# Index and value weights of the sparse mixer loaded in the MLP before it, and its small results in a pool of their own

## The chip, the cores and the metric

The kernel runs on one core of one Trainium2 chip. The metric is the device time of one execution in microseconds. The core has five engines that run their own queues of instructions: TensorE (PE, matrix multiply; PEld is its weight load), VectorE (DVE), ScalarE (ACT), GpSimd (POOL) and SyncE (SP), which here issues nearly all DMAs.

## The reference, cut to what matters

A decoder trunk of four residual layers over x of 512 tokens by 1024 channels, float32: an attention-and-SSM mixer, an MLP, a sparse attention mixer (DSA), a second MLP. Each layer ends in a layer norm. The change lies at the border of the first MLP and the DSA mixer, which picks 128 keys for each query before it attends:

```python
proj = x @ w_in                       # q 1024, k 256, v 256, qi 8x32, ki 32, wi 8 columns
rel = relu(einsum('bqhd,bsd->bqsh', qi_b, ki))           # index: 8 heads of 32
score = einsum('bqsh,bqh->bqs', rel, wi_b) * idx_scale
score = where(causal, score, -inf)
_, idx = top_k(score, 128)            # for each query
... softmax attention over the chosen keys, 16 heads, 4 key heads, ALiBi ...
x = layer_norm(ALPHA * x + o @ w_out)
x = layer_norm(ALPHA * x + square(relu(x @ w1)) @ w2)    # MLP, d_ff 4096
```

## The kernel before, in words

Every float32 product is computed in three float32r matmuls: both operands are split into a rounded part (`hi`, a copy on ACT) and the rest (`lo`, a subtraction on DVE or POOL); `mm3` (lines 129 to 133) adds hi·hi, hi·lo and lo·hi. `weights` (line 96) loads 512 KB of weights into a tile `raw` (three in rotation) and splits it into `whi` and `wlo` (four in rotation in the common pool `wp`; the MLP's pool `hp` has four of its own). x stands transposed and split in `xhi`, `xlo`.

A tile scheduler orders the instructions of each engine when the kernel is built; on the chip each engine then runs its own list strictly in that order, and SP its list of DMAs. A tile's next user waits until its last reader is done.

The MLP (`mlp`) computes 32 column blocks of the hidden layer and folds most of the down projection into products of half matrices (`down_chunk`), with a side sum `u`. Its last two groups of four blocks (`up_split`, with a scratch tile `r`) are followed by `mlp_block` for the four token blocks, and each token block's layer norm (`layer_norm`, with scale and shift in `gb`) follows its last product. The norm parameters are loaded at any time after the tile `gb` is free, here early in the MLP.

The DSA mixer starts with `index_scores`. It loads and splits the small weights of ki and wi (`wk`, 64 columns) and two blocks of qi weights, all in `wp`. For each half of the tokens (c = 0, 1; 256 tokens) it computes three projections `psi` (k of the index with wi, then two of its queries), splits them into `hl` tiles (two in rotation), and sends them through DRAM to another layout: `hl` to `kd` and from there to `kist`, `hl` to `qd` and from there to `qist` (three DMAs), all on SP's queue. Then `score_block` runs for the query blocks 1, 2, 3 (256, 384, 512 keys): eight matmuls `psx` (one for each head), each followed by a ReLU on ACT into `rel` (four in rotation) and one accumulation `acc` on DVE (line 1081). Block 0 needs no choice.

`top_keys` (line 1106) finds the 128 largest scores of each query in 16 steps: `vec.max` gives the next eight (MAX8), `vec.match_replace` strikes them out, and each needs the one before it. It runs for block 1 alone, later for blocks 2 and 3 in turns. `project_v1` loads and splits two weight tiles of v and computes it (`psb`, 96 matmuls of 256 columns); then two projections of k and eight of q follow (`psa`), whose weights from the third q on are split on POOL. The attention (`sparse_attention`) begins with query block 2, whose first DVE instruction (line 1143) reads `dist`, the result of `top_keys`.

Of the kernel before, what the change touches and what calls it, by code (L numbers as in the profile page):

```python
# [8 lines left out]
F32 = mybir.dt.float32  # L9
# [26 lines left out]
class Trunk:  # L36
# [59 lines left out]
    def weights(self, srcs, n=1024, eng=None, pool=None, parts=1, tag=None):  # L96

        nc = self.nc
        raw, hi, lo = self.w_tiles(pool, tag)
# [8 lines left out]
    def w_cols(self, w, c0, eng=None, pool=None, tag=None):  # L108
# [4 lines left out]
        hi, lo = self.weights(srcs, eng=eng, pool=pool, tag=tag)  # L113
        return hi.rearrange("p (k c) -> p k c", c=P), lo.rearrange("p (k c) -> p k c", c=P)
# [90 lines left out]
    def mlp(self, w1, w2, g, b, last):  # L205
# [7 lines left out]
        with self.tc.tile_pool(name=self.nm("mlp"), bufs=2, side="right", reuse_waits="tile") as hp:  # L213
# [17 lines left out]
            def up_split(grp):  # L231
                hhi, hlo = h_tile(F32R), h_tile(F32R)
                for f in range(4):
                    ps = self.proj_fm(w1, grp * 512 + f * P, None)
                    h = hp.tile([P, S], F32, tag="r", bufs=1, name=self.nm("r"))
                    nc.scalar.activation(h, ps, AF.Relu)
                    nc.scalar.activation(h, h, AF.Square)
                    nc.scalar.copy(hhi[:, f, :], h)
                    nc.vector.tensor_tensor(hlo[:, f, :], h, hhi[:, f, :].bitcast(F32), ALU.subtract)
                    yield hhi, hlo  # L240

            for hs in up_raw(0, True):
                pass
            u = hp.tile([P, 2, 512], F32, tag="u", bufs=1, name=self.nm("u"))
# [710 lines left out]
    def mixer_dsa(self, w_in, w_out, g, b):  # L955
        nc, tc = self.nc, self.tc
        act, vec, pool = nc.scalar, nc.vector, nc.gpsimd
        with tc.tile_pool(name="m1", bufs=1, reuse_waits="tile") as mp, \
                tc.tile_pool(name="m1d", bufs=1, space=DRAM) as dp, \
# [6 lines left out]
            for h in range(16):  # L966
                pool.memset(sc[64 * (h % 2):64 * (h % 2) + 64, h // 2:h // 2 + 1], -0.125 / slope(h))
            with tc.tile_pool(name="idxs", bufs=1, side="right", reuse_waits="tile") as sp:
                accs, drm = self.index_scores(w_in, ip, sp, dp)
            vec.tensor_copy(dist[:, 0, 0:P], drm[:, S - P:])  # L970
            self.top_keys((1,), ip, accs, drm, dist)
            self.project_v1(w_in, v)
# [8 lines left out]
            with tc.tile_pool(name="att1", bufs=2, side="right", reuse_waits="tile") as ap:  # L981
                attend = lambda m, qb: self.sparse_attention(m, qb, qsts[4 * m:4 * m + 4], ap, kst, v, dist, chi, clo)
                self.top_keys((2, 3), ip, accs, drm, dist)
# [25 lines left out]
    def index_scores(self, w_in, op, ip, dp):  # L1009
# [3 lines left out]
        drm = op.tile([P, S], F32, name="drm")  # L1013
        cm = op.tile([P, S], F32, name="cm")
# [3 lines left out]
        pool.memset(cm, 0.0)  # L1018
        pool.affine_select(out=cm, in_=cm, pattern=[[-1, S]], compare_op=ALU.is_ge, fill=LOW,
                           base=S - P, channel_multiplier=1)  # L1020


        raw, hi, lo = self.w_tiles()
# [8 lines left out]
        wk = [t[:, 0:n].rearrange("p (k c) -> p k c", c=64) for t in (hi, lo)]  # L1032
        wts = [wk] + [self.w_cols(w_in, 1536 + i * P) for i in range(2)]
        wi = op.tile([P, NB, 8], F32, name="wi")

        kst = ip.tile([96, S], F32R, name="kist")
        qst = ip.tile([96, 8, S], F32R, name="qist")
        for c in range(2):
            tok = slice(c * 256, c * 256 + 256)
            kd = dp.tile([2, 32, 256], F32, name="kd", bufs=2)  # L1040
            qd = dp.tile([2, 2 * P, 256], F32, name="qd", bufs=2)
            for i, (hi, lo) in enumerate(wts):
                m = P if i else 64
                ps = (self.abank([P, 256], "psi") if c == 0 or i == 0 else
                      self.psb.tile([P, 256], F32, tag="psb", name=self.nm("psi")))
                for k in range(KT):
                    self.mm3(ps[:m], hi[:, k, :], lo[:, k, :], self.xhi[:, k, tok], self.xlo[:, k, tok],
                             k == 0, k == KT - 1)
                rows = slice(0, P) if i else slice(32, 64)
                hl = self.hl_tile()[:, :, 0:256]  # L1050
                self.split(hl[rows, 0, :], hl[rows, 1, :], ps[rows])
                if i == 0:
                    nc.sync.dma_start(kd.rearrange("a d t -> d a t"), hl[rows].bitcast(F32))
                    wiT = ip.tile([8, S], F32, tag="rel", bufs=4, name=self.nm("wiT"))[:, 0:256]
                    act.activation(wiT, ps[0:8], AF.Copy, scale=0.0625)
                else:
                    nc.sync.dma_start(qd[:, (i - 1) * P:i * P, :].rearrange("a d t -> d a t"), hl.bitcast(F32))
            nc.sync.dma_start(kst[0:64, tok].bitcast(F32), kd.rearrange("a d t -> (a d) t"))
            nc.sync.dma_start(kst[64:96, tok].bitcast(F32), kd[0])
            for r in range(3):  # L1060
                nc.sync.dma_start(qst[32 * r:32 * r + 32, :, tok].bitcast(F32),
                                  qd[r // 2].rearrange("(h d) t -> d h t", d=32))
# [3 lines left out]
            act.copy(wi[:, 2 * c:2 * c + 2, :], ps)  # L1066
        accs = [None] + [self.score_block(qb, wi, qst, kst, cm, op, ip) for qb in (1, 2, 3)]
        return accs, drm

    def score_block(self, qb, wi, qst, kst, cm, op, ip):  # L1070

        nc = self.nc
        nk = (qb + 1) * P
        qs = slice(qb * P, (qb + 1) * P)
        acc = op.tile([P, S], F32, tag="acc", bufs=3, name=self.nm("acc"))[:, :nk]
        for h in range(8):
            ps = self.abank([P, S], "psx")
            nc.tensor.matmul(ps[:, :nk], qst[:, h, qs], kst[:, :nk], start=True, stop=True)
            r = ip.tile([P, S], F32, tag="rel", bufs=4, name=self.nm("rel"))[:, :nk]
# [3 lines left out]
        return acc  # L1083

    def project_v1(self, w_in, v):

        nc = self.nc
        ws = []
        for i in range(2):
# [4 lines left out]
            ws += [(hi[:, k, :], lo[:, k, :]) for k in range(4)]  # L1094
        for t in range(NB):
# [10 lines left out]
    def top_keys(self, qbs, ip, accs, drm, dist):  # L1106

        vec = self.nc.vector
        for step in range(TOPK // 8):
            for qb in qbs:  # L1110
                acc = accs[qb]
                top = ip.tile([P, 8], F32, tag="top", bufs=1, name=self.nm("top"))
# [42 lines left out]
    def run(self):  # L1155
# [3 lines left out]
        self.mlp(a["w1"][0], a["w2"][0], g[1:2], b[1:2], False)  # L1159
# [42 lines left out]
```

## Time and profile before

| | us |
|---|---|
| median of 3 runs | 1166.77 (1166.69 to 1170.47) |
| the profiled execution | 1165.24 |
| its span, first to last instruction | 1163.5 |
| PE busy in the span | 1108.7 (95%) |
| DVE busy | 841.5 (72%) |
| ACT busy | 532.4 (46%) |
| POOL busy | 173.1 (15%) |

The profile is of one execution; it gives for each engine what ran when, and what ended its idle time. A busy PE counts matmuls in its pipeline. PE is nearly always busy, so the places where it stands still are what to look for: the chain of work that ended last runs over PE for 80% of the span and over DVE for 12%. The first MLP ends at about 590 us, the index runs to about 652 us, the attention from 698 to 790 us.

### The profile page before, as it was taken

The page shows a single profiled execution, that of the slowest core. Times are in us where ns is not written, and L with a number is a line of the kernel's source. Part 1 is how long each engine was busy: PE and PEld are TensorE (multiplying, and loading weights), DVE is VectorE, ACT ScalarE, POOL GpSimd, SP SyncE. Part 2 cuts the span into 40 slices and gives each one's busy share as a digit, 9 for nine tenths or more (in the row PEclk, how much of TensorE's full clock was granted, in tenths as well). Part 3 has the DMA queues.
Part 4 walks back from the last instruction along what each step waited for, and adds up shares of the span by engine and source line. Part 5 has one row for each costly group of instructions (what it writes and reads, how often), then busy time and mean ns, then how long its engine had stood idle before and what let it go on. Part 6 is the DMA issues. An engine that isn't in the chain of part 4 may idle for free.

```text
span 1163.5 us, 15569 instructions
## 1 busy us (share of the span) xinstructions
PE 1108.7 (95%) x5860; PEld 923.6 (79%) x5860; DVE 841.5 (72%) x1255; ACT 532.4 (46%) x832; POOL 173.1 (15%) x201
## 2 busy tenths in 40 slices
PE   7988998999999999999999959998999999999997
PEld 6877876788888888888888847776988888888886
DVE  7997598694666866975668997538548668587736
ACT  5534387324444544554135427642445445445510
POOL 1043230320000000000021744325000000000001
PEclk9999999999999999999999989999999999999999
DMA  7526683751242242333056850025304414415101
GB/s 244 142 64 156 188 220 100 211 151 37 72 145 91 75 150 66 110 108 79 1 141 160 217 164 1 19 69 186 109 19 127 129 35 145 127 38 162 37 1 73
DMA packets 147307, 126.99 MB, mean 109 GB/s; under 512 B 24353, under 2 KB 115297, under 8 KB 147233
## 3 DMA queue, kind: packets, MB, share of 16 engines
q1 hardware_dynamic: 145552, 123.59, 36.7%
q10 hardware_dynamic: 1680, 2.41, 0.6%
q8 instruction: 46, 0.75, 0.3%
q14 instruction: 29, 0.23, 0.1%
HBM read 105.80 MB, written 5.37 MB: 96 GB/s over the span
## 4 chain that ended last, share of the span: by engine, by line
PE 80%; DVE 12%; DMA 3%; issue 2%; ACT 2%; SPq 1%; POOLq 0%; DVEq 0%; ACTq 0%
PE psa L133 11%; PE psa L132 11%; PE psa L131 11%; PE psb L313 7%; PE psb L311 7%; PE psb L312 7%; PE pso L949 3%; PE psb L382 3%; PE psb L381 3%; PE psb L380 2%; PE pst L942 2%; DVE acc L1114 2%; DVE top L1113 2%; PE psb L841 2%; PE psb L842 2%
## 5 line engine op out<-in xcount | busy, mean ns | idle before, releaser
L133 PE MATMUL psa<-xhi,wlo 128*128 128x512 f32 (+1 forms) x720 | 267.1, 372 | 0.0
L132 PE MATMUL psa<-xlo,whi 128*128 128x512 f32 (+1 forms) x720 | 266.6, 371 | 0.0
L131 PE MATMUL psa<-xhi,whi 128*128 128x512 f32 (+1 forms) x720 | 265.6, 371 | 0.2 <-ACT xhi L202 0.2
L104 ACT CAST whi<-raw 128x1024 fp32r<-128x1024 f32 (+1 forms) x129 | 133.3, 1046 | 200.9 <-PE psa L132 130.1
L105 DVE TENSOR_TENSOR wlo<-raw,whi 128x1024 fp32r<-128x1024 f32 (+1 forms) x102 | 127.8, 1258 | 80.5 <-ACT whi L104 79.7
L132 PEld LDWEIGHTS psa<-xlo,whi 128*128 128x128 f32 x720 | 135.7, 188 | 23.4 <-DVE xlo L203 0.4
L133 PEld LDWEIGHTS psa<-xhi,wlo 128*128 128x128 f32 x720 | 135.8, 189 | 23.1
L131 PEld LDWEIGHTS psa<-xhi,whi 128*128 128x128 f32 x720 | 135.0, 188 | 23.1 <-ACT xhi L202 0.5
L299 DVE TENSOR_TENSOR wlo<-b,whi 128x1024 fp32r<-128x1024 f32 x84 | 102.5, 1221 | 43.0 <-ACT whi L298 42.8
L311 PE MATMUL psb<-whi,whi 128*128 128x512 f32 x336 | 130.7, 389 | 0.0
L312 PE MATMUL psb<-wlo,whi 128*128 128x512 f32 x336 | 130.7, 389 | 0.0
L313 PE MATMUL psb<-whi,wlo 128*128 128x512 f32 x336 | 129.7, 389 | 0.0
L298 ACT CAST whi<-b 128x1024 fp32r<-128x1024 f32 x84 | 88.3, 1051 | 42.0 <-PE psb L313 30.2
L105 POOL TENSOR_TENSOR wlo<-raw,whi 128x1024 fp32r<-128x1024 f32 x27 | 70.8, 2632 | 132.5 <-ACT whi L104 131.4
L184 POOL TENSOR_TENSOR rs<-rs,two 128x1 f32<-128x1 f32 x16 | 22.7, 1417 | 423.8 <-DVE rs L183 423.8
L312 PEld LDWEIGHTS psb<-wlo,whi 128*128 128x128 f32 x336 | 63.1, 188 | 13.2
L313 PEld LDWEIGHTS psb<-whi,wlo 128*128 128x128 f32 x336 | 63.1, 188 | 13.1
L311 PEld LDWEIGHTS psb<-whi,whi 128*128 128x128 f32 x336 | 63.1, 188 | 13.0
L293 DVE TENSOR_TENSOR b<-b,b 128x1024 f32<-128x1024 f32 x48 | 63.1, 1320 | 11.4 <-DMA b<-in_w_dram 10.9
L298 ACT CAST whi<-h 128x1024 fp32r<-128x1024 f32 x36 | 38.0, 1054 | 54.0 <-PE psb L312 34.0
L299 DVE TENSOR_TENSOR wlo<-h,whi 128x1024 fp32r<-128x1024 f32 x36 | 43.9, 1220 | 14.0 <-ACT whi L298 13.5
L841 PE MATMUL psb<-whi,xhi 128*128 128x512 f32 x128 | 51.5, 410 | 0.8 <-DVE x L848 0.6
(263 smaller groups left out, 1955.4 us busy)
## 6 DMA issues: line engine op xcount, KB each, us to landing
raw<-in_w_dram SPq DMA_DIRECT2D x80, 512.0 KB, 4.1
b<-in_w_dram SPq DMA_DIRECT2D x48, 512.0 KB, 4.5
raw<-in_w_in_dram SPq DMA_DIRECT2D x29, 512.0 KB, 4.5
raw<-in_w_out_dram SPq DMA_DIRECT2D x16, 512.0 KB, 4.8
qst<-hl SPq DMA_DIRECT2D x48, 128.0 KB, 3.5
kst<-hl SPq DMA_DIRECT2D x24, 256.0 KB, 4.7
gb<-in_ln_g_dram SPq DMA_DIRECT2D x4, 512.0 KB, 4.1
gb<-in_ln_b_dram SPq DMA_DIRECT2D x4, 512.0 KB, 5.0
```

The costliest lines, as they stand in the source:

```text
L104: nc.scalar.copy(hi[:, c], raw[:, c])
L105: (eng or nc.vector).tensor_tensor(lo[:, c], raw[:, c], hi[:, c].bitcast(F32), ALU.subtract)
L131: mm(ps, lhi, rhi, start=start, stop=False)
L132: mm(ps, lhi, rlo, start=False, stop=False)
L133: mm(ps, llo, rhi, start=False, stop=stop)
L293: vec.tensor_tensor(o, p, q, op)
L298: act.copy(hi, src)
L299: vec.tensor_tensor(lo, src, hi.bitcast(F32), ALU.subtract)
L311: mm(ps, lh, bhi[:, k, :], start=i + k == 0, stop=False)
L312: mm(ps, lh, blo[:, k, :], start=False, stop=False)
L313: mm(ps, ll, bhi[:, k, :], start=False, stop=i + k == 2)
L841: nc.tensor.matmul(ps, chi[:, k, tok], whi, start=i == 0, stop=False)
```

## The change

Six things are done, all around the border of the two layers:

- A new pool `idx0` is opened before the first MLP (`index_open`) with `drm` (distances), `kist`, `wi` and `acc1`, the scores of query block 1. `drm` is filled before the MLP.
- `index_early`, called at the MLP's last group, loads and splits the three weight tiles of the index into tiles of the MLP's pool (tags `b22`, `b12`, `b11`), and the two of v into `wp`. `index_projections` is called before the MLP's pool closes.
- Within it, for c = 0 only 128 tokens of the queries are projected (block 1; block 0 is never scored), and the scores of block 1 are computed at once, before the second half of the tokens.
- The split results lie in one tile `hls` for each half (two places, used in turn by the three projections) instead of the rotating `hl`.
- The tile `cm` with the causal bias goes; `score_block` fills each `acc` by one DVE instruction from `drm` and always adds to it.
- In both MLPs `u` and `r` share the one tile of `gb` (`ur`; `r` now has two places), so the norm parameters can be loaded only when both are no longer read.

```diff
-    def mlp(self, w1, w2, g, b, last):
+    def mlp(self, w1, w2, g, b, last, early=None):
...
-                    h = hp.tile([P, S], F32, tag="r", bufs=1, name=self.nm("r"))
+                    h = r[:, f % 2, :]
...
+            ur = self.cp.tile([P, 2, D], F32, tag="gb", bufs=1, name=self.nm("ur"))
+            u, r = (ur[:, i, :].rearrange("p (h c) -> p h c", c=512) for i in range(2))
...
-            u = hp.tile([P, 2, 512], F32, tag="u", bufs=1, name=self.nm("u"))
...
+                    then = early(hp) if early else None
...
+            if early:
+                then()
...
+    def index_open(self):
+        ip = self.ix = self.ctx.enter_context(self.tc.tile_pool(name="idx0", bufs=1, side="right"))
+        self.dp = self.ctx.enter_context(self.tc.tile_pool(name="m1d", bufs=1, space=DRAM))
+        self.drm = ip.tile([P, S], F32, name="drm")
+        self.kist = ip.tile([96, S], F32R, name="kist")
+        self.wi = ip.tile([P, NB, 8], F32, name="wi")
+        self.acc1 = ip.tile([P, 256], F32, name="acc1")
...
+    def index_early(self, w_in, hp):
...
+        def tiles(tag):
+            raw = self.wp.tile([P, 1024], F32, tag="raw", bufs=3, name=self.nm("raw"))
+            return raw, *(hp.tile([P, 1024], F32R, tag=tag, bufs=2, name=self.nm("wx")) for _ in range(2))
...
+        wts += [self.w_cols(w_in, 1536 + i * P, tiles=tiles(tag)) for i, tag in enumerate(("b12", "b11"))]
+        self.vw = self.v1_weights(w_in)
+        return lambda: self.index_projections(wts, hp)
...
+            hls = hp.tile([P, 2, 2, 256], F32R, tag="b21", bufs=2, name=self.nm("hls"))
+            rel = hp.tile([P, 4, 256], F32, tag="s4", bufs=1, name=self.nm("rel"))
...
+                n = P if i and c == 0 else 256
+                at = slice(tok.stop - n, tok.stop)
...
-                hl = self.hl_tile()[:, :, 0:256]
+                hl = hls[:, i % 2, :, 0:n]
...
+            if c == 0:
+                qst = hp.tile([P, 1024], F32R, tag="b21", bufs=2, name="qist1")[0:96].rearrange(
+                    "p (h t) -> p h t", t=P)
+                self.load_index_queries(qst, P)
+                slots = itertools.count()
+                self.score_block(1, qst, self.acc1, lambda: rel[:, next(slots) % 4, :])
...
-            nc.vector.scalar_tensor_tensor(acc, r, wi[:, qb, h:h + 1], acc if h else cm[:, S - nk:],
-                                           ALU.mult, ALU.add)
+        nc.vector.tensor_scalar(acc, self.drm[:, S - nk:], BIG, LOW, ALU.is_ge, ALU.mult)
...
+            nc.vector.scalar_tensor_tensor(acc, r, self.wi[:, qb, h:h + 1], acc, ALU.mult, ALU.add)
...
+        self.index_open()
+        self.mlp(a["w1"][0], a["w2"][0], g[1:2], b[1:2], False, lambda hp: self.index_early(a["w_in1"], hp))
```

The scheduler then orders each engine anew. PE's list is the same, shape by shape, outside the index. Three places of the lists follow. SP, the index's DMAs, before (kd, qd: stores to DRAM of the index's k and queries; kist, qist: loads of them in the other layout; raw: weights):

```order
L1057 DMA qd<-hl_5104 128x2x256
L1061 DMA qist<-qd 32x8x256 x3
L101 DMA raw_5588<-in_w_in_dram 128x8x128
L1053 DMA kd<-hl_5144 32x2x256
L101 DMA raw_5629<-in_w_in_dram 128x8x128
L1057 DMA qd<-hl_5175 128x2x256
L1058 DMA kist<-kd 64x256
L1059 DMA kist<-kd 32x256
L101 DMA raw_5670<-in_w_in_dram 128x8x128
L1057 DMA qd<-hl_5204 128x2x256
L1061 DMA qist<-qd 32x8x256 x3
```

and now:

```order
L1084 DMA qd<-hls_4991 128x2x128
L1102 DMA qist_5084<-qd 32x8x128 x3
L1084 DMA qd<-hls_5123 128x2x256
L1080 DMA kd<-hls_5123 32x2x256
L1086 DMA kist<-kd 64x256
L1087 DMA kist<-kd 32x256
L1084 DMA qd<-hls_5123 128x2x256
L1102 DMA qist<-qd 32x8x256 x3
```

The weight loads between them are gone to earlier places, the first queries are half as many, and in the second half the store of k comes after that of the first queries. PE, around the scores of block 1 (psx), before:

```order
L133 MATMUL psi_5179<-xhi,wlo_5010 128x256
L1078 MATMUL psx_5218<-kist,qist 128x256
L1078 MATMUL psx_5223<-kist,qist 128x256
L1078 MATMUL psx_5228<-kist,qist 128x256
L1065 MATMUL psw_5213<-ident,wiT_5148 128x8 x2
L1078 MATMUL psx_5233<-kist,qist 128x256
L1101 MATMUL psb_5404<-whi_5393,xhi 128x256
```

and now:

```order
L133 MATMUL psi_5182<-xhi,wx_4714 128x256
L1112 MATMUL psx_5089<-kist,qist_5084 128x256
L1112 MATMUL psx_5093<-kist,qist_5084 128x256
L1112 MATMUL psx_5097<-kist,qist_5084 128x256
L1112 MATMUL psx_5101<-kist,qist_5084 128x256
L1112 MATMUL psx_5105<-kist,qist_5084 128x256
L1112 MATMUL psx_5109<-kist,qist_5084 128x256
L1112 MATMUL psx_5113<-kist,qist_5084 128x256
L1112 MATMUL psx_5117<-kist,qist_5084 128x256
L131 MATMUL psi_5125<-xhi,wx_4699 64x256
```

All eight scores now stand together, behind 48 projections of the second half (72 before), and the third 24, those of its k (psi_5125), stand behind the scores. DVE, at the end of block 1's scores (acc) and the start of its `top_keys`, before:

```order
L1081 SCALAR_TENSOR_TENSOR acc_5217<-rel_5250,wi,acc_5217 128x256
L1081 SCALAR_TENSOR_TENSOR acc_5217<-rel_5255,wi,acc_5217 128x256
L1113 MAX top_5342<-acc_5217 128x8
L1114 MATCH_REPLACE acc_5217<-top_5342,acc_5217 128x256
L1113 MAX top_5345<-acc_5217 128x8
```

and now:

```order
L1115 SCALAR_TENSOR_TENSOR acc_2456<-rel_4992,wi,acc_2456 128x256 x8
L860 TENSOR_TENSOR hls_5123<-psi_5125,hls_5123 32x256
L1148 MAX top_5336<-acc_2456 128x8
L1149 MATCH_REPLACE acc_2456<-top_5336,acc_2456 128x256
L1148 MAX top_5339<-acc_2456 128x8
L1149 MATCH_REPLACE acc_2456<-top_5339,acc_2456 128x256
L860 TENSOR_TENSOR hls_5123<-psi_5182,hls_5123 128x256
L1148 MAX top_5342<-acc_2456 128x8
L1149 MATCH_REPLACE acc_2456<-top_5342,acc_2456 128x256
L1148 MAX top_5345<-acc_2456 128x8
L1149 MATCH_REPLACE acc_2456<-top_5345,acc_2456 128x256
L1148 MAX top_5348<-acc_2456 128x8
```

The split of the second half's k now stands between the last accumulation and the first MAX8, and a split of its queries (and, some rows on, two fills of `acc` and a copy into `dist`) stand within block 1's steps.

## Rows read from the trace of the kernel before

**Rows 1.** The waits of PE from 585 to 700 us: sum, count, largest.

```profile
PE psl L1136 <- DVE pst L1143: 14.6, 1, 14.6
```

**Rows 2.** DVE's timeline at five places: start, us, engine, line, operation.

```profile
614.92 2.25 DVE L1081 SCALAR_TENSOR_TENSOR acc<-rel,wi,acc 128x256 f32<-128x256 f32 x4 [0.74 <-ACT rel L1080]
617.21 0.43 DVE L1113 MAX8 top<-acc 128x8 f32<-128x256 f32 x1
...
618.19 0.43 DVE L1113 MAX8 top<-acc 128x8 f32<-128x256 f32 x1
...
653.88 0.69 DVE L1113 MAX8 top<-acc 128x8 f32<-128x512 f32 x1
...
697.74 0.55 DVE L1143 CUSTOM_DVE_ANT_0 pw<-psl,dist 128x384 f32<-128x384 f32 x1
```

**Rows 3.** Busy time by stretch: length, PE, PEld, DVE, ACT, POOL, granted clock, DMA.

```profile
540.00:550.00 10.00, 10.00 (x46) 8.26 (x44) 3.49 (x6) 3.88 (x6) 0.00 (x0) 1.00 0.38 107
...
598.00:604.00 6.00, 6.00 (x54) 5.85 (x52) 1.71 (x3) 1.52 (x4) 0.00 (x0) 1.00 0.59 202
...
608.70:610.20 1.50, 0.09 (x2) 0.12 (x2) 0.50 (x1) 0.97 (x1) 0.00 (x0) 1.00 1.20 231
...
686.00:688.00 2.00, 0.00 (x0) 0.00 (x0) 1.90 (x6) 0.00 (x0) 0.85 (x1) 0.91 0.74 218
```

**Rows 4.** DVE's timeline: the end of the MLP's scratch, its first norm.

```profile
547.63 0.69 DVE L239 TENSOR_TENSOR h<-r,h 128x512 fp32r<-128x512 f32 x1
...
565.34 1.27 DVE L185 SCALAR_TENSOR_TENSOR x<-x,mv,gb 128x1024 f32<-128x1024 f32 x1
```

**Rows 5.** DMA issues, 590 to 626 us: count, KB each, median us to landing.

```profile
qd<-hl SPq DMA_DIRECT2D x4, 256.0 KB, 4.8
...
gb<-in_ln_b_dram SPq DMA_DIRECT2D x1, 512.0 KB, 5.1
kd<-hl SPq DMA_DIRECT2D x2, 64.0 KB, 4.6
```

**Rows 6.** SP's timeline, the index's DMAs: start and length of the issue.

```profile
596.10 0.34 SPq L1053 DMA_DIRECT2D kd<-hl  x1
...
600.54 0.49 SPq L1058 DMA_DIRECT2D kist<-kd  x1
...
602.07 0.37 SPq L1057 DMA_DIRECT2D qd<-hl  x1
604.41 1.31 SPq L1061 DMA_DIRECT2D qist<-qd  x3
...
618.24 1.31 SPq L1061 DMA_DIRECT2D qist<-qd  x3
```

**Rows 7.** ACT's timeline: a weight cast, the split behind kd; PE's: the scores.

```profile
600.56 0.37 ACT L854 CAST hl<-psi 128x256 fp32r<-128x256 f32 x1 [1.11 <-DMA kd<-hl]
...
604.19 1.05 ACT L104 CAST whi<-raw 128x1024 fp32r<-128x1024 f32 x1 [3.18 <-PE psi L132]
...
610.12 0.59 PE L1078 MATMUL psx<-kist,qist 96*128 96x256 f32 x3 [1.41 <-issue]
...
623.86 0.94 PE L1078 MATMUL psx<-kist,qist 96*128 96x384 f32 x4 [1.00 <-DMA qist<-qd]
```

**Rows 8.** DVE from 617.2 to 697.8 us by form: busy, mean ns, idle before.

```profile
L1119 DVE TENSOR_TENSOR dist<-acc,drm 128x256 f32<-128x256 f32 x1 | 2.6, 2592 | 0.0
L105 DVE TENSOR_TENSOR wlo<-raw,whi 128x1024 fp32r<-128x1024 f32 x2 | 2.5, 1226 | 1.3 <-ACT whi L104 1.3
...
L1081 DVE SCALAR_TENSOR_TENSOR acc<-rel,wi,cm 128x384 f32<-128x384 f32 x1 | 0.6, 619 | 0.4 <-ACT rel L1080 0.4
...
L1119 DVE TENSOR_TENSOR dist<-acc,drm 128x384 f32<-128x384 f32 x1 | 0.5, 549 | 0.0
L1118 DVE TENSOR_SCALAR acc<-acc 128x512 f32<-128x512 f32 x1 | 0.4, 420 | 0.0
```

**Rows 9.** Timelines of DVE and of POOL where both subtract.

```profile
638.19 0.74 DVE L1081 SCALAR_TENSOR_TENSOR acc<-rel,wi,acc 128x512 f32<-128x512 f32 x1
...
639.18 2.56 DVE L1081 SCALAR_TENSOR_TENSOR acc<-rel,wi,acc 128x512 f32<-128x512 f32 x1
...
632.33 2.42 POOL L105 TENSOR_TENSOR wlo<-raw,whi 128x1024 fp32r<-128x1024 f32 x1 [36.79 <-ACT whi L104]
...
638.76 2.42 POOL L105 TENSOR_TENSOR wlo<-raw,whi 128x1024 fp32r<-128x1024 f32 x1 [2.43 <-ACT whi L104]
```

More of the change, by code (lines that the diff above doesn't have):

```diff
@@ L106, in weights, with w_cols @@
         return hi, lo
[L108 removed]
+    def w_cols(self, w, c0, eng=None, pool=None, tag=None, tiles=None):
         def srcs(raw):
@@ L967, in mixer_dsa @@
                 pool.memset(sc[64 * (h % 2):64 * (h % 2) + 64, h // 2:h // 2 + 1], -0.125 / slope(h))
+            accs = [None, self.acc1] + [ip.tile([P, S], F32, tag="acc", bufs=2, name=self.nm("acc"))[:, :(qb + 1) * P]
+                                        for qb in (2, 3)]
+            drm = self.drm
             with tc.tile_pool(name="idxs", bufs=1, side="right", reuse_waits="tile") as sp:
-                accs, drm = self.index_scores(w_in, ip, sp, dp)
+                qst = sp.tile([96, 8, 256], F32R, name="qist")
+                self.load_index_queries(qst, 256)
+                for qb in (2, 3):
+                    rel = lambda: sp.tile([P, S], F32, tag="rel", bufs=4, name=self.nm("rel"))
+                    self.score_block(qb, qst[:, :, (qb - 2) * P:(qb - 1) * P], accs[qb], rel)
             vec.tensor_copy(dist[:, 0, 0:P], drm[:, S - P:])
-            self.top_keys((1,), ip, accs, drm, dist)
-            self.project_v1(w_in, v)
+            self.top_keys((1,), accs, drm, dist)
+            self.project_v1(self.vw, v)
             for m in range(2):
@@ L982, in mixer_dsa @@
                 attend = lambda m, qb: self.sparse_attention(m, qb, qsts[4 * m:4 * m + 4], ap, kst, v, dist, chi, clo)
-                self.top_keys((2, 3), ip, accs, drm, dist)
+                self.top_keys((2, 3), accs, drm, dist)
                 qsts += [self.project_q(w_in, mp, pr, sc) for pr in range(4, 8)]
@@ L1053, in index_scores @@
                     nc.sync.dma_start(kd.rearrange("a d t -> d a t"), hl[rows].bitcast(F32))
-                    wiT = ip.tile([8, S], F32, tag="rel", bufs=4, name=self.nm("wiT"))[:, 0:256]
+                    wiT = rel[0:8, 3, :]
                     act.activation(wiT, ps[0:8], AF.Copy, scale=0.0625)
                 else:
[L1057 to L1062, printed above, removed]
+                    nc.sync.dma_start(self.qd[:, (i - 1) * P:i * P, 0:n].rearrange("a d t -> d a t"),
+                                      hl.bitcast(F32))
+            nc.sync.dma_start(self.kist[0:64, tok].bitcast(F32), kd.rearrange("a d t -> (a d) t"))
+            nc.sync.dma_start(self.kist[64:96, tok].bitcast(F32), kd[0])
             ps = self.psb.tile([P, 2, 8], F32, tag="psb", name=self.nm("psw"))
@@ L1065, in index_scores, with load_index_queries, score_block, v1_weights @@
                 nc.tensor.transpose(ps[:, t, :], wiT[:, t * P:(t + 1) * P], self.ident[0:8, 0:8])
[L1066 to L1070, printed above, removed]
+            act.copy(self.wi[:, 2 * c:2 * c + 2, :], ps)
+            if c == 0:
[4 more added lines that the diff above has]
+                self.score_block(1, qst, self.acc1, lambda: rel[:, next(slots) % 4, :])
+    def load_index_queries(self, qst, n):
+        for r in range(3):
+            self.nc.sync.dma_start(qst[32 * r:32 * r + 32].bitcast(F32),
+                                   self.qd[r // 2, :, 0:n].rearrange("(h d) t -> d h t", d=32))
+    def score_block(self, qb, qst, acc, rel):
         nc = self.nc
         nk = (qb + 1) * P
-        qs = slice(qb * P, (qb + 1) * P)
-        acc = op.tile([P, S], F32, tag="acc", bufs=3, name=self.nm("acc"))[:, :nk]
+        nc.vector.tensor_scalar(acc, self.drm[:, S - nk:], BIG, LOW, ALU.is_ge, ALU.mult)
         for h in range(8):
             ps = self.abank([P, S], "psx")
-            nc.tensor.matmul(ps[:, :nk], qst[:, h, qs], kst[:, :nk], start=True, stop=True)
-            r = ip.tile([P, S], F32, tag="rel", bufs=4, name=self.nm("rel"))[:, :nk]
+            nc.tensor.matmul(ps[:, :nk], qst[:, h, :], self.kist[:, :nk], start=True, stop=True)
+            r = rel()[:, :nk]
             nc.scalar.activation(r, ps[:, :nk], AF.Relu)
-            nc.vector.scalar_tensor_tensor(acc, r, wi[:, qb, h:h + 1], acc if h else cm[:, S - nk:],
-                                           ALU.mult, ALU.add)
-        return acc
-    def project_v1(self, w_in, v):
-        nc = self.nc
+            nc.vector.scalar_tensor_tensor(acc, r, self.wi[:, qb, h:h + 1], acc, ALU.mult, ALU.add)
+    def v1_weights(self, w_in):
         ws = []
@@ L1104, in project_v1, with top_keys @@
             nc.scalar.copy(v[:, t, :], o)
-    def top_keys(self, qbs, ip, accs, drm, dist):
+    def top_keys(self, qbs, accs, drm, dist):
         vec = self.nc.vector
@@ L1111, in top_keys @@
                 acc = accs[qb]
-                top = ip.tile([P, 8], F32, tag="top", bufs=1, name=self.nm("top"))
+                top = self.ix.tile([P, 8], F32, tag="top", bufs=1, name=self.nm("top"))
                 vec.max(top, acc)
```

39 lines of the change are left out of this document (17 added, 22 removed).

## The prediction, made before the change was run

> **What bounds the kernel now.** I began with the waits of PE. The page shows PE busy for 95% of the span, so a change can only pay where PE stands still, and between 585 and 700 us, the stretch that the change touches, one wait counts: 14.6 us for DVE's line 1143 [rows 1]. The reader is to see there that DVE, and not the matmuls, decides when the attention starts.
>
> Next I read DVE's timeline backwards from that point [rows 2]. Line 1143 starts at 697.74 us, right behind `top_keys` of blocks 2 and 3, whose first MAX8 is at 653.88; its 16 steps take 2.7 us each (697.74 - 653.88 = 43.9 with the closing operations) and the change doesn't touch them. Ahead lies the stretch from the first MAX8 of block 1 at 617.21 to 653.88, 36.7 us, in which DVE takes the steps of block 1 and the accumulations of blocks 2 and 3 in turns, with only 1.3 + 0.4 us of idle time [rows 8]. So the end of the chain is: the start of the first MAX8, plus the length of this stretch, plus 43.9 us. PE's own work in the index can shrink or shift by some us with no effect, because the 14.6 us swallow it. What counts is by how much the first MAX8 moves and by how much the stretch behind it grows or shrinks.
>
> Last I looked at the MLP's tail, where the change puts its new work: PE is full there, DVE is busy 3.49 and ACT 3.88 of 10 us [rows 3].
>
> **The work moved into the MLP's tail: 0.** Five casts on ACT of at most 1.05 us [rows 7] and five subtractions on DVE of at most 1.23 us [rows 8] are 5.3 and 6.1 us, in a tail of some 40 us in which both engines are idle for more than half. They are covered by PE's matmuls; without that cover they would cost up to 6 us. The norm parameters must now wait until the scratch `r` is read for the last time, 547.63 + 0.69 = 548.3 us, and are first needed at 565.34 [rows 4]. That leaves 17 us for two loads of at most 5.1 us each [rows 5], even one behind the other, so nothing again. The second MLP has the same order of events.
>
> **(a) The first MAX8 comes earlier: -2.3 us.** Before, the path is: store of k issued at 596.10, the loads of `kist` at 600.54 (4.4 us for the store to land), the second store of queries at 602.07 (1.5 later, behind the two `kist` issues), loads of `qist` from 604.41 (2.3 later), first score at 610.12 (5.7 later: three issues of 1.31 us in all, and the landing) [rows 6, 7]. Now:
> - The first store goes out about 0.6 earlier, since a copy on DVE that stood ahead of its split is gone: 595.5. It lands 4.4 later, at 599.9. The second split of queries still waits for that landing, as it did (1.11 us of it are seen on ACT [rows 7]), because three projections share two places.
> - Second store of queries: 599.9 + 1.5 less 0.2 for a shorter split = 601.2; loads of `qist` 2.3 later, 603.5. They carry half the bytes, and no weight load of 512 KB goes out right behind them; I take 4.7 in place of 5.7 for them (bounds: 5.7, and 2.3, what the store of queries took). First score at 608.2 us.
> - Eight accumulations follow at 2.25/4 = 0.56 us [rows 2], without weight splits between them: about 613.4 with the ReLU ahead. DVE then waits for the split of the second half's k, whose 24 matmuls now stand behind the scores: at 6.00/54 = 0.11 us each [rows 3] they end near 613.8, and with the cast and the subtraction MAX8 starts near 614.9. Against 617.21 that is 2.3 earlier (bounds by the landing: 1.3 to 4.0).
>
> **(b) Four short instructions inside the stretch: +1.7 us.** The split of the second half's queries, two fills of `acc` and the copy into `dist` now stand behind the first MAX8. The nearest row is a tensor-scalar of 128x512 at 0.42 us [rows 8]; four of them are 1.7 (bounds: 1.2 if the smaller ones are cheaper, 2.4 by the 0.62 of a first accumulation).
>
> **(c) The wait for the scores of block 2: 0.** DVE now makes ten steps of block 1 ahead of the first accumulation of 384 columns; one step is 618.19 - 617.21 = 0.98 us [rows 2]. It gets there at 614.9 + 9.8 + 1.7 = 626.4. The scores: the second half's k is stored at 615.0, and SP then passes `kist`, the last queries and `qist` in this order: 2.5 for the store, 1.1 for two issues of some 0.5 [rows 6], 2.4 for the queries, 4.9 for `qist` (for the store and `qist` less than the 4.4 and 5.7 of the first half [rows 6, 7], since no weights travel beside them), which makes 625.9. So both arrive nearly together, about 1 us is lost to the ReLUs behind a weight cast, and the 1.7 us of idle time in the stretch [rows 8] stay about what they are. Bounds: all of it goes (-1.7), or the hops take as long as their medians say (the second rival).
>
> **(d) Collisions of DVE with POOL: -2.1 us.** Three accumulations in the stretch take about 1.8 us too long, as the one at 639.18: 2.56 us where the same form took 0.74 at 638.19; POOL's subtraction runs from 638.76 to 641.18 beside it [rows 9]. The subtraction into `dist` takes 2.59 where its wider form takes 0.55 [rows 8]. In all 3 x 1.8 + 2.0 = 7.5 us. Each needs a two-input DVE instruction that meets a long subtraction of POOL; MAX8 and MATCH_REPLACE aren't stretched. The first of POOL's subtractions, at 632.33 [rows 9], will come some 3 us later, since its cast stands behind the ReLUs of block 2, and by my count three instructions meet one instead of four: 5.4 us. Bounds: none (-7.5), or five (+2).
>
> [...]
>
> **Sum.** -2.3 + 1.7 + 0 - 2.1 = -2.7 us against the profiled execution's 1165.24 us: 1162.5. The median of the runs is 1166.77, 1.5 above the profiled one, so the forecast on the median is 1166.77 - 2.7 = **1164.0 us**; its own range is 1161.5 to 1166.5. After the change PE's wait at the start of the attention should still be there, within 3 us of its old size.
>
> **The rivals.**
> 1. *The collisions vanish.* If POOL's subtractions fall beside MAX8 and MATCH_REPLACE only: -2.3 + 1.7 - 7.5 = -8.1, which gives 1158.7. For it: steps and accumulations alternate, so it is a matter of tenths of a us. Against it: a long subtraction of POOL takes 2.42 of every 6.4 us there (632.33 to 638.76 [rows 9]), and 16 accumulations are to pass. Chance 0.12.
> 2. *The second half's transfers become the bound: slower.* They now stand one behind the other on SP, after the scores of block 1. By the medians a store of k takes 4.6, one of queries 4.8 [rows 5], and the later `qist` took 623.86 - 618.24 = 5.6 [rows 6, 7]: 615.0 + 4.6 + 1.1 + 4.8 + 5.6 = 631.1, 4.7 us after DVE gets there. The sum is then +2.0 or, with the ReLUs' delay on top, 1168.9. It decides from an arrival at about 629, where the gain is used up. For it: the hops did take that long in the second half. Against it: weight loads of 512 KB went out between them then, and these are gone. Chance 0.18.
> 3. *TensorE's clock falls in the new gap.* PE has only 48 projections ahead of the scores now and stands still some 2.5 us. A gap of 1.4 us left the granted clock at 1.00, the long one of 14.6 us had brought it to 0.91 between 686 and 688 [rows 3]. [...] Chance 0.11. [...]
> 4. *The early scores aren't early.* If the halved queries land no sooner than before and the clock of the path is the landing of k and the shared places, (a) is 0.6 and the sum +0.0 to -1.0: about 1166.5, no change. Chance 0.09.
>
> **How the numbers follow.** The forecast has 0.50. What a measurement of this kernel tells from no change is about 0.5%, 5.8 us: below 1160.9 or above 1172.6. Faster: all of the first rival and a twentieth of the forecast's cases, 0.15. Slower: the tail of the second rival, when the waits for scores also delay blocks 2 and 3, 0.06. The rest is the same, 0.79. A range of 1159.5 to 1169.5 leaves out half of the first rival and a third of the second with some stray cases, about 0.15 to 0.2.
>
> **What would show it.** In the changed profile: (a) the first score near 608.2 and the first MAX8 near 614.9, after a PE gap of some 2.5 us at full clock; (b) four instructions of about 0.42 us behind it; (c) DVE's idle time up to the first MAX8 of block 2's and 3's common steps below 2 us, with the first score of 384 columns near 626; (d) three stretched two-input instructions; the first norm's parameters landed some 10 us before they are needed, and no new wait of PE in the MLP. The forecast is wrong if PE waits in the MLP's tail, if the first score comes after 610, or if DVE stands still more than 3 us before block 2.

## The result, and the profile after

The changed kernel is slower: 1175.8 us (median of nine runs, 1172.2 to 1177.2) against 1168.4 us, a ratio of 1.0064 with a 95% interval of 1.0050 to 1.0077. The forecast was 1164.0 us, its range ended at 1169.5.

The page of the changed kernel, its head and PE's and DVE's busy time and share:

```profile
span 1173.9 us, 15541 instructions
...
PE 1124.2 (96%) x5860; PEld 929.3 (79%) x5860; DVE 842.0 (72%) x1258; ACT 531.5 (45%) x832; POOL 171.3 (15%) x199
```

PE issues the same 5860 instructions, but is busy for 15.5 us longer than before (1108.7). No engine got new work worth that. Its waits from 520 to 720 us (total, count, longest), to be read against [rows 1]:

```profile
PE psl L1171 <- DVE pst L1178: 10.6, 1, 10.6
PE psx L1112 <- DMA qist<-qd: 2.7, 2, 2.3
PE psw L1090 <- ACT rel L1082: 1.3, 1, 1.3
```

PE waits less than before at the attention, not more. So I cut both traces into stages at PE's first and last matmul of each layer (times worked out from PE's timelines, us):

| | first mixer | MLP 1 | index, to the attention | attention | MLP 2 | span |
|---|---|---|---|---|---|---|
| before | 252.0 | 337.6 | 108.8 | 121.4 | 336.1 | 1163.5 |
| changed | 252.8 | 342.2 | 107.8 | 123.7 | 339.8 | 1173.9 |
| changed, tiles moved back (below) | 252.7 | 337.6 | 108.2 | 121.5 | 336.2 | 1163.8 |

These two executions differ by 10.4 us in span, the medians by 7.4, since the one profiled before was quicker than its median. The loss is in both MLPs, 4.6 and 3.7 us, and the second has none of the moved work. It grows evenly while the down projection runs, at a granted clock of 1.00 in both kernels (300 to 540 us). PE from 300 to 540 us, grouped by form (busy, mean ns, idle before), in the kernel before:

```profile
L131 PE MATMUL psa<-xhi,whi 128*128 128x512 f32 x186 | 72.4, 389 | 0.0
...
L312 PE MATMUL psb<-wlo,whi 128*128 128x512 f32 x167 | 65.0, 389 | 0.0
```

and in the changed one:

```profile
L131 PE MATMUL psa<-xhi,whi 128*128 128x512 f32 x179 | 70.0, 391 | 0.0
L317 PE MATMUL psb<-wlo,whi 128*128 128x512 f32 x168 | 66.5, 396 | 0.0
```

The same matmul of 512 columns takes 7 ns more in the down projection (psb). Its starts, from PE's timeline of the changed kernel, lie 230 to 240 ns apart:

```profile
398.60 0.40 PE L317 MATMUL psb<-wlo,whi 128*128 128x512 f32 x1
398.83 0.39 PE L318 MATMUL psb<-whi,wlo 128*128 128x512 f32 x1
399.07 0.39 PE L316 MATMUL psb<-whi,whi 128*128 128x512 f32 x1
399.30 0.40 PE L317 MATMUL psb<-wlo,whi 128*128 128x512 f32 x1
```

Over the 504 matmuls of psb in an MLP the mean distance of starts is 233.9 ns, before 226.7: 504 x 7.2 = 3.6 us for each MLP. The rest of the first MLP's loss is 0.5 us in the up projections (psa), where most of the nine matmuls behind each switch from psb are slow too (six to eight of them start 228 to 236 ns apart), and 0.4 us in the MLP's last products.

What differs there? The order of the MLPs' matmuls and their shapes are the same, so the places of their operands in SBUF are what is left to compare. Each matmul has a stationary operand, called its weights here, and a moving one of 512 columns. In psa the weights are tiles of w1 and x moves; in psb the weights are pieces of the hidden layer and the tiles of w2 move. Both kinds of weights are split into the common pool, and w2 into the MLP's pool. In the built program the new pool takes 5280 bytes per partition, and `u` and `r`, gone from the MLP's pool, took 6144; together they move `h`, `whi`, `wlo` and the other lower tiles of the MLP's pool up by 864 bytes, `whi` from 128992 to 129856. The weights in the common pool (38368) and x's halves (196576) stay. Before, all of these lie at the same place, 480, within 512 bytes. Now the MLP's tiles lie at 320.

The index came out much as forecast up to its first MAX8. DVE's timeline, against [rows 2, 9]:

```profile
613.96 4.60 DVE L1115 SCALAR_TENSOR_TENSOR acc<-rel,wi,acc 128x256 f32<-128x256 f32 x8 [3.51 <-ACT rel L1114]
...
619.79 0.43 DVE L1148 MAX8 top<-acc 128x8 f32<-128x256 f32 x1
...
641.68 2.27 DVE L1115 SCALAR_TENSOR_TENSOR acc<-rel,wi,acc 128x512 f32<-128x512 f32 x1
...
648.13 1.98 DVE L1153 TENSOR_SCALAR acc<-acc 128x256 f32<-128x256 f32 x1
...
652.00 6.30 DVE L1115 SCALAR_TENSOR_TENSOR acc<-rel,wi,acc 128x512 f32<-128x512 f32 x4
658.33 0.69 DVE L1148 MAX8 top<-acc 128x8 f32<-128x512 f32 x1
...
702.19 0.55 DVE L1178 CUSTOM_DVE_ANT_0 pw<-psl,dist 128x384 f32<-128x384 f32 x1
```

and POOL's:

```profile
640.80 2.60 POOL L105 TENSOR_TENSOR wlo<-raw,whi 128x1024 fp32r<-128x1024 f32 x1 [40.37 <-ACT whi L104]
...
647.21 2.75 POOL L105 TENSOR_TENSOR wlo<-raw,whi 128x1024 fp32r<-128x1024 f32 x1 [2.11 <-ACT whi L104]
```

The reader is to see the first MAX8, 24.8 us after the MLP's last matmul (594.96 us) where it was 27.6 (589.60), and the stretch to the first common MAX8, 38.5 us where it was 36.7. In it, instructions of DVE beside POOL are again too long, two of the four at 652.00 by 3.0 us together.

### The profile page after: what moved, and what is told of

It is laid out like the page before. It is cut to its first block, busy times and chain, and to the rows that moved or that the text cites. A ratio compares the mean times of both kernels' runs of the same rounds, so it can differ in the third digit from the quotient of the medians.

```text
span 1173.9 us, 15541 instructions
## 1 busy us (share of the span) xinstructions
PE 1124.2 (96%) x5860; PEld 929.3 (79%) x5860; DVE 842.0 (72%) x1258; ACT 531.5 (45%) x832; POOL 171.3 (15%) x199
## 4 chain that ended last, share of the span: by engine, by line
PE 80%; DVE 12%; DMA 3%; issue 2%; ACT 1%; SPq 1%; POOL 0%; POOLq 0%; DVEq 0%; ACTq 0%
PE psa L131 11%; PE psa L132 11%; PE psa L133 11%; PE psb L318 7%; PE psb L317 7%; PE psb L316 7%; PE pso L954 3%; PE pst L947 3%; PE psb L387 3%; PE psb L386 3%; PE psb L385 3%; PE psb L846 2%; DVE acc L1149 2%; PE psl L1171 2%; PE psb L847 2%
## 5 line engine op out<-in xcount | busy, mean ns | idle before, releaser
L105 DVE TENSOR_TENSOR wlo<-raw,whi 128x1024 fp32r<-128x1024 f32 (+1 forms) x100 | 125.3, 1259 | 74.8 <-ACT whi L104 73.6
L318 PE MATMUL psb<-whi,wlo 128*128 128x512 f32 x336 | 132.5, 397 | 0.0
L303 ACT CAST whi<-b 128x1024 fp32r<-128x1024 f32 x84 | 88.0, 1048 | 45.0 <-PE psb L318 33.9
L317 PEld LDWEIGHTS psb<-wlo,whi 128*128 128x128 f32 x336 | 63.0, 188 | 15.5
```

The lines of the kernel that those rows point to most:

```text
L303: act.copy(hi, src)
L317: mm(ps, lh, blo[:, k, :], start=False, stop=False)
L318: mm(ps, ll, bhi[:, k, :], start=False, stop=i + k == 2)
```

## The experiments

Theories: *addresses* (the places of a matmul's two operands set its pace) against *scratch* (`u` and `r` in the place of the norm parameters slow the MLPs); then, for the index, *gap* (PE's pause before the scores) against *meetings* (DVE held up beside POOL). Place means the start of a tile within 512 bytes.

**1. The tiles moved back.** The changed kernel with

```
+            hp.tile([P, 88], F32, tag="pad", ...)      # 352 bytes, never used
```

> The changed kernel with an unused tile of 352 bytes per partition in the MLP's pool, which moves the pool's tiles h, b11, b12, whi and wlo down so that each starts at the same place within 512 bytes as in the kernel before (480; in the changed kernel 320); order and work are the same. Address theory: the 504 matmuls of each down projection (psb) start 227 ns apart again as before, in place of 231 to 238; each MLP gets back about 4.5 us, the time falls from 1175.8 by 8 to 10 us to about 1166.5, even with or a little below the kernel before. Scratch theory (u and r in the place of the norm parameters slow the matmuls): starts stay 231 to 238 ns apart, time within 1 us of 1175.8.

Measured: 1167.1 us, ratio to the kernel before 0.9989 (0.9980 to 0.9997). PE from 300 to 540 us:

```profile
L317 PE MATMUL psb<-wlo,whi 128*128 128x512 f32 x168 | 65.4, 389 | 0.0
```

An unused tile takes away the whole loss. Scratch falls, since `u` and `r` lie where the change put them.

**2. The kernel before, tiles moved away.** `hp.tile([P, 40], ...)`, 160 bytes, is all that differs from it.

> The kernel before with an unused tile of 160 bytes per partition in the MLP's pool: h, b11, b12, whi, wlo and u start 160 bytes lower, at place 320 within 512 bytes as in the changed kernel; nothing else differs. Address theory: the matmuls of psb start 231 to 238 ns apart, each MLP takes 4.5 us more, time 1168.4 + 9 = about 1177. Scratch theory: no change, 1168.4 within 1 us, starts 227 ns apart.

Measured: 1177.1 us, ratio 1.0079 (1.0067 to 1.0092), with the same group as the changed kernel has:

```profile
L312 PE MATMUL psb<-wlo,whi 128*128 128x512 f32 x165 | 65.3, 396 | 0.0
```

The loss is made without any part of the change. Both MLPs take 342.1 and 340.4 us.

**3 to 5. Other places.** As in 1, with 8, 56 and 24 elements.

> The changed kernel with 32 bytes in place of 352: the tiles start at place 288 within 512, which is the old place modulo 64 but not modulo 128 or more. If only the place within 64 bytes counts, starts are 227 ns apart and both MLPs take what they took before (about 1166.5); if the place within 128 or more bytes counts, they stay 231 to 238 ns apart and the time near 1175.

> The changed kernel with 224 bytes in place of 352: the tiles start at place 96 within 512, the old place modulo 128 but not modulo 256. If the place within 64 or 128 bytes decides, about 1166.5 and starts 227 ns apart; if that within 256 or 512 does, near 1175 and 231 to 238 ns.

> The changed kernel with 96 bytes in place of 352: the MLP's tiles start at place 224 within 512 bytes, the old place modulo 256. If the place within 256 bytes decides, psb starts 227 ns apart and the time is about 1167; if that within 512, it is slowed like 288 (229.7 ns measured), 96 (232.9) and 320 (233.9), and the time lies between 1171 and 1177.

Measured, one run each: 1176.2, 1173.1 and 1168.1 us. The last, 256 bytes from the old place, in the group of psb:

```profile
L317 PE MATMUL psb<-wlo,whi 128*128 128x512 f32 x168 | 65.4, 389 | 0.0
```

So 512 bytes, as I had put it, is too much: the place within 256 bytes decides. The time of 32 bytes holds a first mixer of 257.5 us with four falls of the clock (the mean granted clock of the profiled run is 0.979, in the other runs 0.982 to 0.988), 3 to 7 us more than in the other runs; the MLPs tell more than the time there.

**6. Weights moved as well.** `cp.tile([P, 80], ...)` becomes `[P, 40]`.

> The changed kernel with the first unused tile (320 bytes, at the bottom of all) cut to 160 bytes: the weights in the common pool go to place 320 within 512 bytes, where the MLP's tiles lie in the changed kernel; x's halves xhi and xlo stay at 480. If the distance between the two operands of a matmul within 512 bytes decides: the matmuls of psb (weights of the common pool against tiles of the MLP's pool, now both at 320) start 227 ns apart again, and those of psa (weights at 320, x at 480) get slower instead, to about 234: the MLPs gain 7 us and lose 10 or more, and the other projections lose too, so about 1185. If the place of the moving operand alone decides: psb stays at 234, psa at 227, time near 1176.

Measured: 1177.3 us in one run, and the two groups have changed roles:

```profile
L131 PE MATMUL psa<-xhi,whi 128*128 128x512 f32 x179 | 71.0, 397 | 0.0
...
L317 PE MATMUL psb<-wlo,whi 128*128 128x512 f32 x168 | 65.6, 390 | 0.0
```

The distance of the two operands decides, not the place of one. (I had counted psa's loss too high: the 672 up-projection matmuls of 512 columns in an MLP, 7 ns each, are 5 us.) The table joins these runs (distance is moving operand less weights, modulo 256; the mean distance of starts and the lengths of the MLPs are worked out from PE's timelines):

| kernel | weights at | MLP's tiles at | distance | psb starts, ns | MLP 1, 2, us |
|---|---|---|---|---|---|
| before | 480 | 480 | 0 | 226.7 | 337.6, 336.1 |
| changed | 480 | 320 | 96 | 233.9 | 342.2, 339.8 |
| changed + 352 | 480 | 480 | 0 | 226.7 | 337.6, 336.2 |
| before + 160 | 480 | 320 | 96 | 233.9 | 342.1, 340.4 |
| changed + 32 | 480 | 288 | 64 | 229.7 | 339.8, 337.6 |
| changed + 224 | 480 | 96 | 128 | 232.9 | 341.2, 339.4 |
| changed + 96 | 480 | 224 | 0 | 226.7 | 337.6, 336.1 |
| changed, weights moved | 320 | 320 | 0 (psa: 160) | 227.6 | 342.9, 341.2 |

Within the changed kernel it shows too: of the MLP's last products (line 385), 88 with distance 0 start 227.6 ns apart, 30 with distance 160 start 233.6 (two more, at 314 ns, are left out). With 256 columns it doesn't show: the first up projections have distance 160 in the changed kernel and 0 in run 1, and start 117.9 and 119.8 ns apart.

**7. k's projection first.** As in 1, and the second half's projection of k takes its PSUM tile elsewhere, so that it runs ahead of block 1's scores:

```
-                ps = (self.abank([P, n], "psi") if c == 0 or i == 0 else
+                ps = (self.abank([P, n], "psi") if c == 0 else
```

> The changed kernel with the 352 bytes (1167.1 by the first runs), and the second half's projection of the index's k takes its PSUM tile from the pool of the queries, so that its 24 matmuls run ahead of the scores of block 1 and not behind them. Gap theory (the pause of PE before the scores of block 1, in which the clock fell, and the late store of k cost the index its gain): the pause shrinks from 2.3 us to under 1, the clock stays at its upper level there, the first MAX8 comes 1 to 2 us earlier, DVE's idle time behind it falls from 2.6 us to about 1: about 1164.5 us. Rival (DVE's meetings with POOL eat what is gained): the stretched instructions add up to more than 7.6 us, time stays within 1 us of 1167.1.

Measured: 1160.0 us, ratio 0.9929 (0.9914 to 0.9943), more than either theory had. The clock fell all the same, behind the scores, where PE now waits 3.6 us. Its windows (length, PE, PEld, DVE, ACT, POOL, granted clock, DMA):

```profile
612.00:616.00 4.00, 0.51 (x5) 0.30 (x3) 3.44 (x9) 1.87 (x6) 0.00 (x0) 0.94 0.40 128
616.00:622.00 6.00, 5.85 (x28) 5.83 (x29) 5.66 (x21) 0.28 (x3) 0.00 (x0) 0.50 0.58 134
```

DVE's timeline tells where the gain is,

```profile
640.29 0.74 DVE L1115 SCALAR_TENSOR_TENSOR acc<-rel,wi,acc 128x512 f32<-128x512 f32 x1
...
645.44 0.69 DVE L1148 MAX8 top<-acc 128x8 f32<-128x512 f32 x1
```

beside POOL's:

```profile
640.55 2.75 POOL L105 TENSOR_TENSOR wlo<-raw,whi 128x1024 fp32r<-128x1024 f32 x1 [43.42 <-ACT whi L104]
```

The last accumulation starts before POOL's first subtraction, so none is held up. The first MAX8 comes 1.0 us earlier than in run 1 (24.1 us after the MLP for 25.1), as the gap theory had it, but the stretch behind it takes 29.7 us in place of 38.6: 6.3 us fewer of stretched instructions, 1.7 us less idle time. The index takes 97.2 us in place of 108.2; the attention gives back 4 us (125.8), whose cause I didn't follow.

**8. ReLU in place in PSUM.** As in 1, and for blocks 2 and 3 `r = ps[:, :nk]`.

> The changed kernel with the 352 bytes; the ReLU of the scores of blocks 2 and 3 is written in place in PSUM, so that the accumulations on DVE read one operand from SBUF and one from PSUM. Meeting theory (a DVE instruction waits for POOL's subtraction only where it reads two operands from SBUF): the four stretched accumulations, 5.3 us too long in all, become normal, the fill-in and the subtraction behind block 1 stay stretched by up to 2.3; the attention starts 4 to 5 us earlier: about 1163 us. Rival 1 (any traffic of DVE is held up beside POOL): no change, 1167. Rival 2 (held PSUM tiles delay PE's scores): DVE's idle time in the stretch grows, 1167 or more.

Measured: 1164.6 us, ratio 0.9967 (0.9954 to 0.9981). DVE from 615 to 652.3 us, by form:

```profile
L1115 DVE SCALAR_TENSOR_TENSOR acc<-psx,wi,acc 128x512 f32<-128x512 f32 x8 | 6.0, 748 | 4.4 <-ACT psx L1114 4.0
L1115 DVE SCALAR_TENSOR_TENSOR acc<-psx,wi,acc 128x384 f32<-128x384 f32 x8 | 4.9, 607 | 2.3 <-ACT psx L1114 2.2
```

All sixteen have their normal length, though POOL subtracts beside them. Of the 7.1 us of stretching that go in all, 4.9 come back as idle time (7.6 us in the stretch, 2.7 in run 1), most of it behind the scores, so both the meetings and rival 2 are there.

**9. Without three of POOL's subtractions.** As in 1; for q blocks 2 to 4 `nc.scalar.copy(lo, raw)` stands in their place, so the rest of these weights isn't computed.

> The changed kernel with the 352 bytes, but the rest (lo) of the weights of q blocks 2, 3 and 4 isn't computed by POOL's subtraction: a copy on ACT writes the tile instead, so these three subtractions are left out. Meeting theory: the three stretched DVE instructions that meet them (1.5, 1.7 and 2.2 us too long) become normal, those that meet POOL's shorter subtraction of hl (0.6 to 0.9 each) stay; 7.6 us of stretching become about 2.5, the attention starts 4 to 5 us earlier, about 1163. Rival (DVE is delayed by the scores, not by POOL): the idle time grows by what the meetings lose, time within 1 us of 1167.

Measured: 1161.1 us, ratio 0.9951 (0.9937 to 0.9964). Stretched instructions fall from 7.6 to 1.35 us, and PE's wait at the attention to 5.6:

```profile
PE psl L1171 <- DVE pst L1178: 5.6, 1, 5.6
```

The scheduler also put some steps of block 1 elsewhere, and the first MAX8 comes 1.4 us earlier than in run 1. The stretch behind it is 4.7 us shorter (33.9 for 38.6), and the ratios of the two runs differ by 0.0038, 4.4 us; so the price of these three meetings is nearer 4.5 us than the 6.0 that the medians differ by.

**10 and 11. The wait behind the scores.** The kernel of 7 with `wiT` in free rows of the k tile. In 10 its transposes still came after the split of the last queries, which writes those rows first: the head weights are then values of the queries (the amount of work is the same), and the transposes wait for that split. In 11 they stand right behind k's split.

> The kernel with k's projection first (1160.0), and the transposed head weights wiT lie in the free rows of the k tile of the halves and not in the last of the four places of the ReLUs. Gap theory: PE's wait of 3.6 us for them behind block 1's scores goes, and the clock doesn't fall there (it was at its lower level for 6.8 us): the scores of block 2 come earlier, PE reaches the attention 3 to 5 us earlier; if DVE is ready by then, about 1156 to 1158 us. Rival (DVE is the bound again as soon as PE is early): PE's wait at the start of the attention comes back with 2 to 4 us and the time stays within 1.5 us of 1160.

> The kernel with k's projection first (1160.0), with wiT in the free rows of the k tile and its transposes issued right behind k's split, ahead of the query splits, so that the weights of the heads are the reference's. PE's list now has the 48 query projections of the second half between the scores of block 1, and no wait for the places of the ReLUs. Gap theory: no pause of PE over 2 us behind block 1's scores and no fall of the clock between 600 and 640 us; index stage 2 to 4 us shorter than the 97.2 us of the kernel with k first, about 1157 us. Rival (the order of DVE's accumulations against POOL's subtractions decides): stretched DVE instructions add up to 4 us or more in place of 1.3, PE waits at the attention again, 1160 or more.

Measured: 1162.4 us (0.9964, 0.9950 to 0.9977) and 1165.3 us (0.9986, 0.9977 to 0.9995), both slower than 7. In 11 the clock stays up, as this window shows:

```profile
600.00:640.00 40.00, 36.32 (x254) 33.62 (x253) 26.83 (x64) 16.09 (x38) 4.10 (x2) 1.00 0.39 106
```

But a pause is left: PE's waits have one of 2.7 us, for the split of k, now ahead of the scores:

```profile
PE psw L1085 <- ACT hls L1082: 2.7, 1, 2.7
```

Two rows of DVE's timeline there:

```profile
636.24 2.07 DVE L1115 SCALAR_TENSOR_TENSOR acc<-rel,wi,acc 128x512 f32<-128x512 f32 x1 [0.77 <-ACT rel L1114]
...
648.76 2.41 DVE L1115 SCALAR_TENSOR_TENSOR acc<-rel,wi,acc 128x512 f32<-128x512 f32 x1
```

The forecast of the gap theory fails: without the pause behind the scores and without the fall of the clock the kernel is 5 us slower than run 7. In the scheduler's new order stretched instructions grow to 5.9 us again (5.0 in run 10, 1.3 in run 7), and PE waits 10.9 us at the attention. What the pause alone costs stays open, since the order changed with it. Run 7 is the fastest version and beats both kernels.

## Why the prediction was wrong

**The step that failed** is the term of the sum for the two MLPs, put at 0: "The work moved into the MLP's tail: 0", and for the second "the same order of events". It asked only whether the moved work is covered, and took the MLPs' own matmuls as unchanged without a reason: the order of PE's list was compared, the places of its operands weren't. As to the moved work the 0 holds (with the tiles moved back, MLP 1 takes 337.6 us as before, casts, subtractions and late norm parameters included). But the pool that makes room for it slows the matmuls of both MLPs: 4.6 + 3.7 us, and by runs 1 and 2 about 9 us of the whole. None of the four rivals named it. Runs 1 and 2 show it from both sides.

**(a) came out in size, partly by luck**: forecast -2.3, measured 24.8 - 27.6 = -2.8 in the changed kernel and 25.1 - 27.6 = -2.5 in run 1. These are single executions; runs 3 to 5 have 25.2 to 26.0, and run 2, in the order of before, 29.1. SP's timeline of the changed kernel, against [rows 6]:

```profile
600.90 0.37 SPq L1080 DMA_DIRECT2D kd<-hls  x1
...
606.43 0.49 SPq L1086 DMA_DIRECT2D kist<-kd  x1
...
609.48 1.31 SPq L1102 DMA_DIRECT2D qist<-qd  x3
```

The store of k takes 5.5 us, not 4.4; `qist` comes 3.7 us after its issue began, where I had 4.7 (613.15 for the first score), and the two cancel. Two more errors cancel behind the first score: my times leave 3.0 us for the eight scores (613.8 less 24 x 0.11, against 608.2), which took 2.0 (613.15 to 615.19), and 2.6 for k's 24 matmuls, which took 3.7 (to 618.91), the first of them at a granted clock of 0.50. (My bound of 4.0 for (a) is a wrong sum: 2.3 in place of 4.7 for the landing gives 4.7.)

**(b)** was 1.3 us for 1.7: 0.42, 0.68 for the two fills together and 0.22.

**(c)** was +0.4: DVE idles 2.6 us in the stretch for 2.2 before, by the same count. The second rival, slow transfers, didn't happen.

**(d) failed.** Three meetings and 5.4 us were forecast; there are six and 7.6 us, as much as before (7.55). Three of them are with long subtractions of POOL and cost 5.4 us, as forecast, though not the ones that I had counted: a tensor-scalar with a single input (1.98 us where it took 0.29) is among them, which I had taken to be safe, so two inputs aren't needed. MAX8 and MATCH_REPLACE kept their length, as forecast: in the kernel before MAX8 of 384 columns took 0.56 us with POOL at rest (655.40) and 0.56 beside its subtractions (658.17), MATCH_REPLACE of 384 columns 0.54 beside one (656.08) and 0.54 with POOL done (689.30). Tenths of a us decide such meetings: an accumulation that began 0.05 us behind POOL's subtraction took 2.90 us here (653.70), one that began 0.26 ahead of it kept its 0.74 in run 7. The other three, 2.2 us, are with POOL's shorter subtraction of `hl`, which the term had left out. One of them, in DVE's timeline and in POOL's:

```profile
644.21 1.44 DVE L1115 SCALAR_TENSOR_TENSOR acc<-rel,wi,acc 128x512 f32<-128x512 f32 x1
```

```profile
643.36 1.74 POOL L869 TENSOR_TENSOR hl<-ev,hl 128x512 fp32r<-128x512 f32 x1
```

Run 9 agrees: without three long subtractions 1.35 us of stretching are left, beside the short ones. The index therefore got -2.8 + 1.9 = -0.9 us up to the first common MAX8, in place of -2.7 (the 1.9 are 38.5 - 36.7, mostly (b) and (c)). Run 1 gives -0.11% or -1.2 us, so with the MLPs as before the forecast's sign was right; in the profiles its index is 0.6 us shorter. PE's wait at the attention, which was to stay within 3 us of 14.6, fell to 10.6: DVE is ready 1.0 us earlier after the MLP, and PE gets there 3.1 us later.

**The clock** (third rival) did fall in the new pause, and again longer after the wait at the attention. Windows of the changed kernel:

```profile
613.40:616.80 3.40, 3.40 (x16) 3.25 (x16) 2.42 (x5) 2.64 (x8) 0.00 (x0) 0.50 0.00 0
...
702.80:709.00 6.20, 6.20 (x25) 6.11 (x26) 4.26 (x19) 4.99 (x16) 3.56 (x7) 0.50 0.11 33
```

and of the one before:

```profile
698.40:701.30 2.90, 2.90 (x10) 2.81 (x11) 2.90 (x13) 2.89 (x9) 0.31 (x1) 0.50 0.00 0
```

The first fell on the eight scores and the first eight of k's 24 matmuls, which took 1.1 us more than forecast (the first of k's start 213 ns apart, those behind them 117); behind the accumulations DVE stood still for k's split for 0.8 us. The second is 6.2 us at a granted clock of 0.50 in place of 2.9; at half the pace the 3.3 us more are worth some 1.6 us of the attention's 2.3, by estimate. In run 1, with the same work and order, it is 3.5 us, so that part varies from run to run. (The 0.91 that the prediction read at this wait [rows 3] is a mean over the moment of the fall; from 687.60 to 698.30 us it was 0.50.)

The first rival, meetings that vanish, is what run 7 brings for the most part, by 24 matmuls put earlier: 1.3 us of stretching are left.

## What to carry to other kernels

A pool that is opened, closed or resized can move the tiles beyond it (here by 864 bytes), so compare addresses as well as order: where a long row of matmuls of 512 columns streams from one pool and takes its weights from another, as here in float32r, keep the two at the same place within 256 bytes, if need be with an unused tile (226.7 to 227.6 ns from start to start in these runs, elsewhere 229.7 to 233.9). A loss that is spread evenly over an untouched stage, at unchanged clock and with no idle time, is a sign of it; look at the distance of starts of one form. And meetings of two engines weren't to be forecast here from the order of one: count all instructions of the other engine, the short ones too, give a range both ways, or take the operand away (PSUM; 0.75 us for each accumulation of 512 columns in run 8) or finish the short work before the other engine starts.

## What the runs showed of the hardware

- A matmul of 512 columns of float32r starts 227 ns after the one before where its two operands in SBUF lie at a distance of 0 modulo 256 bytes, 230 to 234 ns (mean of psb) at 64, 96 and 128, and 233.6 ns at 160 (the last products of the MLP in the changed kernel; psa at 160 in run 6 is 397 ns long for 389); the granted clock was 1.00 in both kernels where these were read. At 256 columns no such loss shows (117.9 ns at 160, 119.8 at 0). So the pace depended here on where the weights lie against the moving operand. Why it does, and why most of some nine matmuls after a slow group are slow too, stays open.
- DVE's accumulation of two SBUF operands took up to 2.90 us (653.70 in the changed kernel) where it started beside a running subtraction of POOL, and 0.75 us (mean of eight, run 8) with one operand in PSUM. Where the accumulation started first it kept its 0.74 us (640.29 in run 7), and POOL's subtraction took 2.75 us for its usual 2.4. A tensor-scalar with a single SBUF input took 1.98 us beside POOL's subtraction (648.13 in the changed kernel) and 0.29 without one (650.04 in the kernel before), so that two operands in SBUF, as the theory of run 8 has it, aren't the whole condition; no run shows what is.
